# Residual rows loaded behind a one-column memset, and the first product's additions moved into the second product, in a two-layer encoder trunk on one core

## The chip, the core and the metric

The kernel runs on one core of a Trainium2 chip. The core has five engines that run side by side: TensorE (PE in the profile, with PEld for its weight loads), VectorE (DVE), ScalarE (ACT), GpSimd (POOL) and SyncE (SP). SP and POOL issue the transfers here; SP's go through the hardware queue, POOL's through the software queue. The metric is the time of one execution on the device in microseconds: a median of 2541.53 us over three runs (2537.37 to 2542.77).

## The reference

The trunk has two post-norm layers on 1024 positions of width 1024. After each mixer and after each SwiGLU stands a product, a scaled residual and a layer norm; these four places are what the change is about:

```python
    for layer in range(DEPTH):
        if layer % 2 == 0:
            y = even_mixer(x, ...)      # latent attention + Fourier mixing, @ w_out
        else:
            y = odd_mixer(x, ...)       # gMLP spatial gating, @ odd_w_out
        x = layer_norm(DN_ALPHA * x + y, mix_ln_g[layer], mix_ln_b[layer])
        x = layer_norm(DN_ALPHA * x + swiglu(x, ...), ffn_ln_g[layer], ffn_ln_b[layer])
```

`y` is (pages of width 1024) @ (weights): 12 pages of 128 rows for the even mixer, 16 for the odd one, 22 for each SwiGLU. Everything is float32.

## The kernel before

Each of the four products `x = LN(ALPHA * resid + H @ W)` is one call of `reduce` (lines 409 to 594): mix (stage "mix"), ffn0, odd and ffn1, in that order. The product is made from 2x2 blocks with seven half-size products instead of eight, each called a pass p; `source` (line 382) says which sums of pages and of weights a pass multiplies. The page sums SA, SB and weight sums TA, TB are made earlier and kept in device memory (`job`, `direct`, `page_sums`). A float32 matmul is done as three (`mm3`, lines 141 to 143) on operands split into a high part (`xoh`, a cast on ScalarE, line 135) and a low part (`xol`, a subtraction on VectorE, line 136).

Passes run in the order 1, 5, 6, 4, 7, 2, and 3 at the end. A pass has n groups of up to two pages; (p, g) is group g of pass p, and n is 3 in mix, 4 in odd and 6 in ffn0 and ffn1, where the first group has one page. `load(p, g)` brings both sides of a group with SP transfers into six `rx` buffers and splits them into six pairs of cells; then four row blocks s of 128 rows each take 6 matmuls of 512 columns. A group of two pages is 24 matmuls. The first two groups of pass 1 are loaded before the call (`lead`).

The residual rows go into eight tiles `xt[half, s]` of 128x1024 (512 KB each), named x, q, q, y for half 0 and x four times for half 1. Their tags are those of tiles that the stage before has just used: q is TA and TB, x is the last pages and their sums SA and SB. `residual` loads them with POOL transfers; `gained` multiplies them by the last norm's gain and adds its bias (lines 469 and 470, not in mix); `add` adds a product from a PSUM bank (line 457 for the first addition, which scales by ALPHA, line 459 for the others).

The order on each engine is set by a scheduler that takes instructions by priority (in the order of the code) as soon as its own model has them ready; the engine then runs them in that order and waits at the first that is not ready. `behind(mark)` holds an instruction behind a mark in that order; `self.marks[2]` is the VectorE half of the last split of the stream. A transfer issued by POOL whose tile is still being read holds POOL's queue; a VectorE instruction that writes such a tile holds VectorE's.

Of the kernel before, what the change touches and what calls it, by code (L numbers as in the profile page):

```python
# [112 lines left out]
class Trunk:  # L113
# [295 lines left out]
    def reduce(self, st, resid, rgb, ln, keep, pre=None, left=()):  # L409


        nc, a = self.nc, self.a
        lo, hi = self.LO, self.HI
# [3 lines left out]
        n = len(groups)  # L417
# [16 lines left out]
        token = lambda half, s: s // 2 * 4 + half * 2 + s % 2  # L434
        xt = {(1, s): self.m_tile("x") for s in range(4)}
# [4 lines left out]
        def load(p, g):  # L440
            if (p, g) not in ops:
                ops[p, g] = self.stream(st, p, groups[g], raws, pairs)

        def mm(p, g, s):
            if p in (6, 7):
                acc[p, s] = acc[1 if p == 6 else 6, s]
            elif (p, s) not in acc:
                acc[p, s] = self.bank((4 if p in (1, 3) else 0) + s)
            (hh, hl), (uh, ul) = ops[p, g]
            for i, m in enumerate(groups[g]):  # L450
                c, r = slice(i * 512 + s * P, i * 512 + (s + 1) * P), slice(i * 512, (i + 1) * 512)
                self.mm3(acc[p, s], (hh[:, c], hl[:, c]), (uh[:, r], ul[:, r]), m == 0 and p not in (6, 7), m == M - 1, p in (6, 7))

        def add(half, s, c, p, first=False, op=ALU.add):
            x = xt[half, s][:, c]
            if first:
                nc.vector.scalar_tensor_tensor(x, x, ALPHA, acc[p, s], ALU.mult, op)
            else:
                nc.vector.tensor_tensor(x, x, acc[p, s], op=op)

        def residual(half):
            for s in range(4):
                nc.gpsimd.dma_start(xt[half, s], resid[token(half, s)])

        def gained(half, s):
            if rgb is not None:
                x = xt[half, s]
                with self.behind(self.marks[2]):
                    nc.vector.tensor_tensor(x, x, rg, op=ALU.mult)
                    nc.vector.tensor_tensor(x, x, rb, op=ALU.add)  # L470

        def stat(half, s, c):
            if (half, s) not in stats:
                stats[half, s] = self.small.tile([P, 2, 6], F32, tag="st", name=self.name("st"))
            nc.vector.bn_stats(stats[half, s][:, c, :], xt[half, s][:, c * 512:(c + 1) * 512])  # L475
# [43 lines left out]
        def normed1(s):  # L519
            for c in range(2):  # L520
                stat(1, s, c)
            norm(1, s)


        def spread(jobs, k, of):
            i0, i1 = len(jobs) * k // of, len(jobs) * (k + 1) // of
            for j in jobs[i0:i1]:
                j()
        slots = range(4)
        for p in (1, 5, 6, 4, 7, 2):  # L530
            for g in range(n):
                load(p, g)
                if p == 1 and g == 1:
                    load(1, 2)
                    if rgb is not None:
                        rg, rb = (self.bcast(tmp(), a["ln_" + x][rgb[0], rgb[1]]) for x in "gb")
                    residual(0)
                    last = self.job(st, M - 1, True) if st is self.stage["mix"] else None
                if p == 5 and g == 0:
                    residual(1)  # L540
                if p == 6 and g == 0 and keep is None:
                    fg, fb = (self.bcast(self.raw_tile(), a["ln_" + x][ln[0], ln[1]]) for x in "gb")
                if p == 4 and g == 0 and pre is not None:
                    with self.behind(*self.marks):
                        pre()
                if p in (1, 5) and g > 1:
                    spread([lambda s=s: gained(p == 5, s) for s in slots], g - 2, n - 2)
                if p == 2:
                    spread([lambda s=s: normed1(s) for s in slots], g, n)
                for s in slots:  # L550
                    mm(p, g, s)
                    if p == 1 and s % 2 == 1 and left:
                        left.pop(0)()
                    if g == n - 1:
                        if p == 1:
                            add(0, s, lo, p, True)
                        elif p == 5:
                            add(0, s, hi, p, True)
                            add(1, s, hi, p, True)
                        elif p == 6:  # L560
                            add(0, s, hi, p)
                        elif p == 4:
                            add(1, s, lo, p, True, ALU.subtract)
                        elif p == 7:
                            add(1, s, lo, p)
                            add(1, s, hi, p)
                        else:
                            add(0, s, lo, p)
                            stat(0, s, 0)
                if (p, g) == (5, 0) and last is not None:  # L570
                    last(self.marks[2])
# [837 lines left out]
```

## Time and profile before

| | us |
|---|---|
| median of three runs | 2541.53 |
| the profiled execution | 2541.83 |
| its span | 2540.0 |
| PE busy | 2456.4 (97%) |
| DVE busy | 1808.9 (71%) |
| ACT busy | 1111.1 (44%) |
| POOL busy | 318.5 (13%) |

The span is 1.83 us shorter than the execution's own time. Busy PE counts matmuls that overlap in its pipeline, so 97% does not say how often TensorE waits; the chain and the timeline do. The four calls of `reduce` take their first groups near 560 us (mix), 1122 (ffn0), 1690 (odd) and 2304 (ffn1). Times in the rows are microseconds from the start of the span.

### The profile page before, as it was taken

The numbers are of one execution on the slowest core, as the hardware profiler recorded it, in microseconds if no ns is written. First come the engines' busy times: TensorE is split into PE (matmuls) and PEld (weight loads), VectorE is DVE, ScalarE is ACT, GpSimd is POOL, SyncE is SP. The second block draws the span as 40 slices with busy tenths as digits, with TensorE's granted clock in tenths as the row PEclk, the third lists the DMA queues.
The fourth block names the chain that finished last, engine by engine and source line by source line (L and its number), as shares of the span: only waits on it lengthen the run. The fifth ranks groups of instructions, "written<-read, shape, count | busy, mean of one in ns | idle before, by whom it ended". The sixth has DMA issues, their size and how long they took to land.

```text
span 2540.0 us, 33155 instructions
## 1 busy us (share of the span) xinstructions
PE 2456.4 (97%) x12294; PEld 2073.4 (82%) x12294; DVE 1808.9 (71%) x2537; ACT 1111.1 (44%) x1711; POOL 318.5 (13%) x527
## 2 busy tenths in 40 slices
PE   8989999998999999999999999988989999999997
PEld 6778888887878888887889998877878888887885
DVE  4348878767886776768678776768777676677667
ACT  3235555544553333333456446653463333333331
POOL 1000111010111111110002132430011111111001
PEclk9999999998999999999999999999999999999998
DMA  4122333138334444467654554667624444549553
GB/s 175 43 89 71 130 110 125 57 138 282 138 118 174 169 168 162 168 252 251 226 182 172 202 203 137 195 244 276 224 73 163 177 166 155 177 164 329 190 188 140
DMA packets 164329, 431.95 MB, mean 170 GB/s; under 512 B 20136, under 2 KB 26952, under 8 KB 164168
## 3 DMA queue, kind: packets, MB, share of 16 engines
q1 hardware_dynamic: 108216, 232.11, 27.8%
q0 software_dynamic: 55952, 197.73, 20.9%
q8 instruction: 96, 1.57, 0.2%
q14 instruction: 65, 0.53, 0.1%
HBM read 286.64 MB, written 138.41 MB: 167 GB/s over the span
## 4 chain that ended last, share of the span: by engine, by line
PE 81%; DVE 6%; issue 5%; DMA 4%; ACT 2%; POOL 1%; SPq 1%; DVEq 0%; ACTq 0%; POOLq 0%
PE b L142 18%; PE b L141 18%; PE b L143 18%; PE S L1316 6%; PE b L912 5%; PE mm L141 4%; PE mm L142 4%; PE mm L143 4%; PE mm L1335 2%; DVE xol L136 1%; DMA rx<-h 1%; PE b L848 1%; DMA x<-xs 1%; ACT xoh L135 1%; DVE st L475 1%
## 5 line engine op out<-in xcount | busy, mean ns | idle before, releaser
L135 ACT CAST whi<-raw 128x1024 fp32r<-128x1024 f32 (+3 forms) x277 | 261.2, 951 | 383.4 <-PE b L142 240.2
L135 ACT CAST xoh<-rx 128x1024 fp32r<-128x1024 f32 (+1 forms) x252 | 244.5, 1011 | 413.5 <-PE b L142 308.8
L141 PE MATMUL b<-xoh,whi 128*128 128x512 f32 x1040 | 410.7, 396 | 7.9 <-ACT xoh L135 7.9
L136 DVE TENSOR_TENSOR wlo<-raw,whi 128x1024 fp32r<-128x1024 f32 (+3 forms) x277 | 303.4, 1099 | 159.3 <-ACT whi L135 157.1
L142 PE MATMUL b<-xol,whi 128*128 128x512 f32 x1040 | 406.8, 391 | 0.0
L143 PE MATMUL b<-xoh,wlo 128*128 128x512 f32 x1040 | 406.4, 391 | 0.0
L136 DVE TENSOR_TENSOR xol<-rx,xoh 128x1024 fp32r<-128x1024 f32 (+1 forms) x252 | 287.6, 1168 | 166.0 <-ACT xoh L135 160.3
L142 PE MATMUL b<-xol,xoh 128*128 128x512 f32 x960 | 379.4, 395 | 22.3 <-DVE xol L136 22.3
L141 PE MATMUL b<-xoh 128*128 128x512 f32 x960 | 376.1, 394 | 8.5 <-ACT xoh L135 8.5
L143 PE MATMUL b<-xoh,xol 128*128 128x512 f32 x960 | 377.5, 393 | 0.0
L141 PEld LDWEIGHTS b<-xoh,whi 128*128 128x128 f32 x1040 | 196.6, 189 | 50.3 <-ACT xoh L135 8.8
L142 PEld LDWEIGHTS b<-xol,xoh 128*128 128x128 f32 x960 | 183.1, 191 | 63.3 <-DVE xol L136 25.5
L143 PEld LDWEIGHTS b<-xoh,wlo 128*128 128x128 f32 x1040 | 196.3, 189 | 41.3
L142 PEld LDWEIGHTS b<-xol,whi 128*128 128x128 f32 x1040 | 196.5, 189 | 40.4 <-issue 0.5
L141 PEld LDWEIGHTS b<-xoh 128*128 128x128 f32 x960 | 182.9, 190 | 47.6 <-ACT xoh L135 9.3
L143 PEld LDWEIGHTS b<-xoh,xol 128*128 128x128 f32 x960 | 183.1, 191 | 38.2
L663 ACT COPY y<-b 128x512 f32<-128x512 f32 x200 | 116.6, 585 | 192.7 <-PE b L143 186.1
L141 PE MATMUL b<-xah,whi 128*128 128x512 f32 x416 | 162.5, 391 | 1.3 <-ACT xah L135 1.3
L142 PE MATMUL b<-xal,whi 128*128 128x512 f32 x416 | 162.0, 389 | 0.0
L143 PE MATMUL b<-xah,wlo 128*128 128x512 f32 x416 | 161.9, 389 | 0.0
L131 DVE TENSOR_TENSOR raw<-raw,raw 128x512 f32<-128x512 f32 (+1 forms) x174 | 128.5, 739 | 28.2 <-DMA raw<-w_up 24.7
L708 DVE TENSOR_TENSOR y<-b,y 128x512 f32<-128x512 f32 x84 | 58.0, 690 | 82.9 <-PE b L143 82.6
(378 smaller groups left out, 4590.9 us busy)
## 6 DMA issues: line engine op xcount, KB each, us to landing
raw<-w_gate SPq DMA_DIRECT2D x44, 512.0 KB, 3.6
raw<-w_up SPq DMA_DIRECT2D x44, 512.0 KB
q<-w_down POOLq DMA_DIRECT2D x44, 512.0 KB, 5.3
h<-x POOLq DMA_DIRECT2D x44, 512.0 KB, 3.7
rx<-h SPq DMA_DIRECT2D x60, 256.0 KB, 3.0
rx<-w_down SPq DMA_DIRECT2D x60, 256.0 KB, 4.3
raw<-o_v SPq DMA_DIRECT2D x16, 512.0 KB, 6.1
x<-o_out POOLq DMA_DIRECT2D x16, 512.0 KB, 5.7
```

Of the source, the lines that this page charges most:

```text
L131: self.nc.vector.tensor_tensor(out, a, b, op=ALU.subtract)
L135: a = self.nc.scalar.copy(hi, src)
L136: return a.ins, self.nc.vector.tensor_tensor(lo, src, hi.bitcast(F32), op=ALU.subtract).ins
L141: mm(ps, lh, rh, start=start, stop=False, skip_group_check=skip)
L142: mm(ps, lh, rl, start=False, stop=False, skip_group_check=skip)
L143: mm(ps, ll, rh, start=False, stop=stop, skip_group_check=skip)
L475: nc.vector.bn_stats(stats[half, s][:, c, :], xt[half, s][:, c * 512:(c + 1) * 512])
L663: nc.scalar.copy(t, ps)
L708: self.last_v = nc.vector.tensor_tensor(sb, ps, sb, op=op).ins
L912: nc.tensor.matmul(ps[:, i * 256:(i + 1) * 256], l[:, b, k, c], r[:, k, :], start=start and k == 0 and i == 0 and m == 0, stop=k == 3 and ...
L1316: nc.tensor.matmul(sc[:, kb, :], l[:, s], r[:, kb * 512:(kb + 1) * 512], start=i == 0, stop=i == 4)
L1335: nc.tensor.transpose(ps[:, k, :], p[:, kt * P:(kt + 1) * P], self.ident)
```

## The change

```diff
-        def residual(half):
-            for s in range(4):
-                nc.gpsimd.dma_start(xt[half, s], resid[token(half, s)])
+        def residual(half, s):
+
+            with self.behind(self.marks[2]):
+                nc.vector.memset(xt[half, s][:, 0:1], 0.0)
+            nc.gpsimd.dma_start(xt[half, s], resid[token(half, s)])
...
-                    residual(0)
                     last = self.job(st, M - 1, True) if st is self.stage["mix"] else None
-                if p == 5 and g == 0:
-                    residual(1)
+                if p == 1 and 0 < g < 3:
+                    for s in (2 * g - 2, 2 * g - 1):
+                        residual(0, s)
+                if (p == 1 and g == n - 1) or (p == 5 and g == 0):
+                    for s in (0, 1) if p == 1 else (2, 3):
+                        residual(1, s)
...
-                if p in (1, 5) and g > 1:
-                    spread([lambda s=s: gained(p == 5, s) for s in slots], g - 2, n - 2)
+                if p == 1 and g > 1:
+                    spread([lambda s=s: gained(0, s) for s in slots], g - 2, n - 1)
+                if p == 5 and g == 0:
+                    spread([lambda s=s: gained(0, s) for s in slots], n - 2, n - 1)
+                if p == 5 and g > 0:
+                    spread([lambda s=s: gained(1, s) for s in slots], g - 1, n - 1)
+                if (p, g) == (5, 1):
+                    for s in slots:
+                        add(0, s, lo, 1, True)
...
                     if g == n - 1:
-                        if p == 1:
-                            add(0, s, lo, p, True)
-                        elif p == 5:
+                        if p == 5:
                             add(0, s, hi, p, True)
                             add(1, s, hi, p, True)
...
-                        else:
+                        elif p == 2:
                             add(0, s, lo, p)
                             stat(0, s, 0)
```

Each load of a residual row block now follows a memset of its tile's first column on VectorE, which `behind` puts after the splits of the group at hand; the load overwrites the column. There are 32 memsets, eight in a call, on line 464; the loads stand on line 465 and `gained` on 471 and 472 of the changed kernel. The first additions of pass 1 move from the end of pass 1 to the start of group (5, 1).

On VectorE in ffn0, before, from the multiplication of the first row block on (q_9756 and q_9757 are row blocks (0,1) and (0,2), x_9755 is (0,0); the splits of rx_9879 and rx_9884 are those of group (1, 4), the ones of rx_9915 and rx_9920 those of (1, 5)):

```order
L469 TENSOR_TENSOR q_9756<-q_9756,gb_9785 128x1024
L320 TENSOR_TENSOR x_9736<-x_9715,x_9735 128x512
L470 TENSOR_TENSOR q_9756<-q_9756,gb_9787 128x1024
L469 TENSOR_TENSOR x_9755<-x_9755,gb_9785 128x1024
L136 TENSOR_TENSOR xol<-rx_9879,xoh 128x1024
L470 TENSOR_TENSOR x_9755<-x_9755,gb_9787 128x1024
L136 TENSOR_TENSOR xol<-rx_9884,xoh 128x1024
L469 TENSOR_TENSOR q_9757<-q_9757,gb_9785 128x1024
L136 TENSOR_TENSOR xol<-rx_9915,xoh 128x1024
```

The same place in the changed kernel (the row block (0,0) is x_9763, the splits of (1, 4) are those of rx_9889 and rx_9894, of (1, 5) those of rx_9925 and rx_9930):

```order
L464 MEMSET x_9763 128x1
L136 TENSOR_TENSOR xol<-rx_9889,xoh 128x1024
L320 TENSOR_TENSOR x_9744<-x_9723,x_9743 128x512
L136 TENSOR_TENSOR xol<-rx_9894,xoh 128x1024
L471 TENSOR_TENSOR q_9764<-q_9764,gb_9793 128x1024
L472 TENSOR_TENSOR q_9764<-q_9764,gb_9795 128x1024
L136 TENSOR_TENSOR xol<-rx_9925,xoh 128x1024
L471 TENSOR_TENSOR x_9763<-x_9763,gb_9793 128x1024
L136 TENSOR_TENSOR xol<-rx_9930,xoh 128x1024
L472 TENSOR_TENSOR x_9763<-x_9763,gb_9795 128x1024
```

Both splits of (1, 4) now stand ahead of every multiplication, and the one of (0,0) stands between the two splits of (1, 5). On POOL the load of (0,0), which stood ahead of the stores of SA and SB, stands behind both. ffn1 has the same order.

On VectorE in odd, before, from the last page sum on (line 457 is the first addition of pass 1 for the four row blocks; rx_15031 is the second split of group (5, 0), whose first stood fourteen rows earlier, rx_15068 and rx_15073 are (5, 1), rx_15102 is (5, 2)):

```order
L320 TENSOR_TENSOR x_14624<-x_14624,x_14623 128x512
L457 SCALAR_TENSOR_TENSOR x_14828<-x_14828,b_14832 128x512
L457 SCALAR_TENSOR_TENSOR q_14829<-q_14829,b_14839 128x512
L457 SCALAR_TENSOR_TENSOR q_14830<-q_14830,b_14858 128x512
L457 SCALAR_TENSOR_TENSOR y_14831<-y_14831,b_14865 128x512
L136 TENSOR_TENSOR xol<-rx_15031,xoh 128x1024
L136 TENSOR_TENSOR xol<-rx_15068,xoh 128x1024
L136 TENSOR_TENSOR xol<-rx_15073,xoh 128x1024
L136 TENSOR_TENSOR xol<-rx_15102,xoh 128x1024
```

The changed kernel there (rx_15047 is the second split of (5, 0), with the first right ahead of it, rx_15088 the first of (5, 1); x_14842 is row block (1,2), whose tile is read by the store of SA until it has landed):

```order
L136 TENSOR_TENSOR xol<-rx_15047,xoh 128x1024
L317 TENSOR_TENSOR x_14640<-x_14639,x_14640 128x512
L471 TENSOR_TENSOR q_14845<-q_14845,gb_14926 128x1024
L318 TENSOR_TENSOR x_14639<-x_14639 128x512
L472 TENSOR_TENSOR q_14845<-q_14845,gb_14928 128x1024
L319 TENSOR_TENSOR x_14639<-x_14640,x_14639 128x512
L471 TENSOR_TENSOR q_14846<-q_14846,gb_14926 128x1024
L320 TENSOR_TENSOR x_14640<-x_14640,x_14639 128x512
L472 TENSOR_TENSOR q_14846<-q_14846,gb_14928 128x1024
L471 TENSOR_TENSOR y_14847<-y_14847,gb_14926 128x1024
L464 MEMSET x_14842 128x1
L136 TENSOR_TENSOR xol<-rx_15088,xoh 128x1024
```

The splits of (5, 0) now stand ahead of the page sums and of the multiplications, and those of (5, 1) behind them and behind two memsets. Further on, the eight additions of pass 5 stand ahead of both splits of (6, 0), where before one split stood ahead of them and the other after the fourth.

On TensorE in mix, before, at the end of group (5, 1) (b_5738, b_5745, b_5752 and b_5759 are the banks of pass 5 for row blocks 0 to 3, b_5626 is the one of passes 1 and 6 for row block 0):

```order
L143 MATMUL b_5759<-xoh,xol 128x512
L141 MATMUL b_5626<-xoh 128x512
L141 MATMUL b_5738<-xoh 128x512
L142 MATMUL b_5738<-xol,xoh 128x512
L141 MATMUL b_5745<-xoh 128x512
L142 MATMUL b_5745<-xol,xoh 128x512
L141 MATMUL b_5752<-xoh 128x512
```

The changed kernel there (b_5742, b_5749, b_5756 and b_5763 are the banks of pass 5, b_5626, b_5633, b_5640 and b_5647 those of passes 1 and 6):

```order
L143 MATMUL b_5763<-xoh,xol 128x512
L141 MATMUL b_5626<-xoh 128x512
L142 MATMUL b_5626<-xol,xoh 128x512
L143 MATMUL b_5626<-xoh,xol 128x512
...
L141 MATMUL b_5647<-xoh 128x512
L141 MATMUL b_5742<-xoh 128x512
L142 MATMUL b_5742<-xol,xoh 128x512
L141 MATMUL b_5749<-xoh 128x512
```

One matmul of (6, 0) stood ahead of those of (5, 2); now 19 of its 24 do. On VectorE the first additions of pass 1 stand behind the splits of (5, 0) and of (5, 1) there, and all eight memsets behind those of (1, 2).

## Rows read from the trace of the kernel before

**Rows 1.** The page: the chain that ended last, by engine.
```profile
PE 81%; DVE 6%; issue 5%; DMA 4%; ACT 2%; POOL 1%; SPq 1%; DVEq 0%; ACTq 0%; POOLq 0%
```

**Rows 2.** Timeline of PE: start, duration, instruction [idle before it <-what ended it].
```profile
572.08 0.79 PE L141 MATMUL b<-xoh 128*128 128x512 f32 x1 [3.53 <-ACT xoh L135]
...
597.85 0.80 PE L141 MATMUL b<-xoh 128*128 128x512 f32 x1 [4.96 <-ACT xoh L135]
...
1147.44 0.79 PE L142 MATMUL b<-xol,xoh 128*128 128x512 f32 x1 [5.67 <-DVE xol L136]
...
1224.69 0.50 PE L142 MATMUL b<-xol,xoh 128*128 128x512 f32 x1 [0.94 <-DVE xol L136]
...
1701.16 0.79 PE L848 MATMUL b<-q,whi 128*128 128x128 f32 x2 [8.93 <-ACT whi L839]
...
1735.58 0.79 PE L142 MATMUL b<-xol,xoh 128*128 128x512 f32 x1 [6.55 <-DVE xol L136]
...
2328.05 0.79 PE L142 MATMUL b<-xol,xoh 128*128 128x512 f32 x1 [5.18 <-DVE xol L136]
...
2496.12 0.65 PE L142 MATMUL b<-xol,xoh 128*128 128x512 f32 x1 [1.80 <-DVE xol L136]
```

**Rows 3.** Timeline of PE in ffn0, before and after its wait.
```profile
1141.15 0.39 PE L143 MATMUL b<-xoh,xol 128*128 128x512 f32 x1
1141.38 0.39 PE L141 MATMUL b<-xoh 128*128 128x512 f32 x1
...
1149.31 0.63 PE L143 MATMUL b<-xoh,xol 128*128 128x512 f32 x1
1149.74 0.63 PE L141 MATMUL b<-xoh 128*128 128x512 f32 x1
```

**Rows 4.** Timeline of DVE in ffn0.
```profile
1142.76 1.23 DVE L469 TENSOR_TENSOR x<-x,gb 128x1024 f32<-128x1024 f32 x1 [4.64 <-DMA x<-xs]
1143.90 1.22 DVE L136 TENSOR_TENSOR xol<-rx,xoh 128x1024 fp32r<-128x1024 f32 x1
```

**Rows 5.** Timeline of POOL in ffn0.
```profile
1132.68 0.53 POOL L463 DMA_DIRECT2D x<-xs  x1
...
1137.28 0.54 POOL L349 DMA_DIRECT2D ffn0SB<-x  x1 [1.65 <-DVE x L320]
```

**Rows 6.** DMA queues, 1135 to 1139: packets, MB, share of 16 engines.
```profile
q0 software_dynamic: 303, 1.11, 67.9%
q1 hardware_dynamic: 304, 0.56, 36.1%
```

**Rows 7.** Timeline of DVE in ffn1.
```profile
2323.37 1.23 DVE L469 TENSOR_TENSOR x<-x,gb 128x1024 f32<-128x1024 f32 x1 [4.53 <-DMA x<-xs]
```

**Rows 8.** DMA issues, 1137.6 to 1138: KB, us from issue to landing.
```profile
ffn0SB<-x POOLq DMA_DIRECT2D x1, 512.0 KB, 8.6
```

**Rows 9.** Timeline of DVE in odd.
```profile
1726.10 0.69 DVE L317 TENSOR_TENSOR x<-x,x 128x512 f32<-128x512 f32 x1 [1.93 <-DMA tp<-x]
...
1732.51 1.28 DVE L457 SCALAR_TENSOR_TENSOR q<-q,b 128x512 f32<-128x512 f32 x2
1733.70 0.69 DVE L457 SCALAR_TENSOR_TENSOR y<-y,b 128x512 f32<-128x512 f32 x1
```

**Rows 10.** Timeline of ACT in mix.
```profile
570.98 1.04 ACT L135 CAST xoh<-rx 128x1024 fp32r<-128x1024 f32 x1 [2.06 <-DMA rx<-w_out]
...
596.75 2.94 ACT L135 CAST xoh<-rx 128x1024 fp32r<-128x1024 f32 x3 [8.47 <-DMA rx<-mixSB]
```

**Rows 11.** DMA queues, 566 to 572.
```profile
q0 software_dynamic: 402, 1.51, 61.7%
q1 hardware_dynamic: 537, 0.98, 42.4%
```

**Rows 12.** Timeline of POOL in mix.
```profile
587.99 0.54 POOL L341 DMA_DIRECT2D mixSB<-raw  x1 [1.19 <-DVE raw L320]
```

**Rows 13.** Timeline of POOL in odd.
```profile
1732.30 0.54 POOL L862 DMA_DIRECT2D oddSB<-x  x1 [1.20 <-DVE x L320]
...
1735.50 0.53 POOL L463 DMA_DIRECT2D x<-xs  x1 [1.26 <-DMA oddSB<-x]
```

## The prediction, made before the result was known

> **What bounds the kernel now.** First the chain on the page: TensorE carries 81% of it [rows 1], so a time changes only where TensorE waits. Then TensorE's timeline, read for idle time ahead of a matmul. In the four calls of `reduce` (I call them mix, ffn0, odd, ffn1 after their stage) six long waits stand [rows 2]: mix 3.53 and 4.96 us, ffn0 5.67, odd 8.93 and 6.55, ffn1 5.18. After a wait of 1.8 us or more the matmuls come 0.43 us apart instead of 0.23 [rows 3], which is 1.2 GHz instead of 2.4; after one of 0.94 us they do not stay slow [rows 2]. About nine matmuls are slow each time, 9 x 0.2 + 0.2 = 2.0 us. So the six waits cost 34.8 us and 12 us of slow clock with them.
>
> Why they wait, in ffn0: VectorE's `gained` multiply of row block (0,0) stood 4.64 us for its load, and the split that TensorE needed stands right behind it [rows 4]. The load was issued at 1132.68 [rows 5], landed at 1142.7. In that stretch the software queue (POOL's) and the hardware queue (SP's) together fill the 16 engines: shares 67.9% and 36.1% [rows 6]. ffn1 has the same wait, 4.53 us [rows 7].
>
> **ffn0 and ffn1.** The change puts `gained` of (0,0) one group later: behind both splits of group (1,4), as the second order piece shows, so (1,4) runs without a wait. But its load now stands behind the stores SA and SB on POOL, issued with SB at 1137.3 instead of 1132.7 [rows 5]: seventh in the software queue instead of fifth. That queue moves 1.11 MB in 4 us, 278 GB/s, 1.89 us for 524 KB [rows 6]. So it lands at 1142.7 + 2 x 1.89 = 1146.5 (from below: SB, seventh today, landed 8.6 us after its issue, 1145.9 [rows 8]; from above: rival A).
> The second split of (1,5) stands behind that multiply: 1146.5 + 1.14 + 1.23 = 1148.9 (spacing of two such VectorE rows: 1.14 [rows 4]). TensorE wants it after 24 matmuls of (1,4) and one more: 1141.4 + 25 x 0.227 = 1147.05. New wait 1.85 us. Then VectorE has nine instructions of 1024 columns, two of 512 (0.60 each [rows 9]) and four memsets from the landing to the second split of (5,1): 9 x 1.14 + 2 x 0.6 + 4 x 0.1 = 11.9, so 1158.4. No row shows a memset of one column: between 0 and the 0.60 of a 512-wide instruction; I take 0.1, near the low end. Today that point of TensorE comes 60 matmuls after 1147.44: 1147.44 + 60 x 0.227 + 2.0 = 1163.06. Now it comes at 1158.4, or at 1159.1 if the 1.85 us also slow the clock. Gain 4.0 to 4.7, I take 4.4.
> ffn1 by the same steps: landing 2323.3 + 3.8 = 2327.1, split 2329.5, TensorE there at 2328.05 - 5.18 + 24 x 0.227 = 2328.3, wait 1.2 us, no slow clock; VectorE's chain ends at 2339.0, today 2328.05 + 60 x 0.227 + 2.0 = 2343.7. Gain 4.7.
>
> **mix.** Here the splits wait for the stream itself: for the second load of group (1,2), cast at 570.98 [rows 10]. Between 566 and 572 the residual rows on the software queue took 1.51 MB and the stream 0.98 [rows 11]. Seven of the eight row loads now go behind that group's splits. The stream's load has to come 4.8 us earlier to be cast and split (1.05 + 1.24) before TensorE asks at 572.08 - 3.53 = 568.55. With more than half of the traffic ahead of it gone I take that as reached.
> The second wait hangs on the last page's sums: store SB issued at 587.99 [rows 12], the reload cast at 596.75 [rows 10], 8.8 us for a store and a load, 4.4 each. After the change the sums are made earlier (near 577), but the store stands behind eight row loads: issue from 567, first landing near 571, then 524 KB at 1.51 MB per 6 us [rows 11], 2.08 us each, so the eighth at 585.6, SB tenth at 589.8, reload 594.2, TensorE 1.1 later (as 597.85 after 596.75): 595.3. Meanwhile it has (1,2), (5,0), (5,1): 568.55 + 72 x 0.227 = 584.9, and 19 matmuls of (6,0), which the new order puts ahead of (5,2): 589.2. So 6.1 us of wait remain. The end of (5,2) and (6,0): 595.3 + 29 x 0.227 + 2.0 = 603.9, today 597.85 + 47 x 0.227 + 2.0 = 610.5. Gain 6.6. If the software queue had the engines alone (2.49 MB in the 6 us [rows 11], 1.26 us each) SB would be back at 586.7, nothing would wait, end 595.8, gain 14.7. If the first load came no earlier, nothing is gained. I take 8, near the value that rests on today's shares.
>
> **odd.** The 8.93 us wait for ScalarE, which waits for the stream's load; one row load of 512 KB leaves that stretch, 524 KB at 415 GB/s [rows 11] = 1.3 us at most; I take 1. The 6.55 us go: the splits of (5,0) move ahead of the `gained` work (third and fourth order pieces). What is late next: VectorE's work from the page sums on. Its first sum starts at 1726.1, when the store of the page has landed [rows 9]; to the second split of (5,1) there are 4 x 0.6 + 8 x 1.14 + 2 memsets = 11.7, so 1737.8, and TensorE, through (5,0) at 1734.3, waits 3.6. Six more items and four adds bring (5,2) to 1744.7 (wait 1), and the eight adds of pass 5 now stand ahead of both splits of (6,0): 1749.3 + 4 x 1.14 + 8 x 0.6 + 2 x 1.14 = 1761.0, while TensorE arrives at 1755.9: a wait of 5 us and 2 of slow clock, 1763.0. Today the same matmul comes 96 after 1735.58: + 21.8 + 1.6 = 1759.0. So 4 lost, 1 gained: +3. Between -6 (nothing of the chain is late) and +7 (the two new memsets between the sums and the split also wait for stores SA and SB; today such a store took 3.2 us [rows 13], which they just pass).
>
> **The 32 memsets, the doubled adds and the line moves** cost nothing else: the number of `gained` and add instructions is the same; 32 x 0.1 = 3 us on VectorE, which is busy 71%; where they sit in its queue they are priced above.
>
> **Sum.** 8 + 4.4 + 4.7 - 3 = 14.1. The profiled execution took 2541.83, its span 2540.0 and 1.83 around it; the median of the runs is 2541.53, so it needs no correction. 2541.8 - 14.1 = 2527.7, I say 2528.
>
> **Rivals.**
> A. The wait only moves to a later load (no change). The splits of (1,4) are made earlier in ffn0, so their buffers come free and SP refills the hardware queue at once. If the software queue then had half the bytes, 205 GB/s, 2.56 us each: the first of the seven lands at 1142.7 - 4 x 1.89 = 1135.1, the seventh six later at 1150.5, VectorE's chain ends at 1162.4, today 1163.06: 0.6 gained, the same in ffn1. In mix SB would be tenth at 571 + 9 x 2.56 = 594, restart 599.5, gain 2.4. With odd at +3 the time is 2541. Against it: both queues had work in 1135 to 1139, and the software queue still had two thirds of the bytes [rows 6]. The Trainium skill, "DMA: Bandwidth & Descriptors", section "Queues, rings and completion order", says that a DMA engine serves its queues in turn, a whole packet from one before it goes to the next, which speaks for A if packets are alike. In the row the numbers of packets are alike and the packets are not: 303 carried 1.11 MB and 304 carried 0.56 MB [rows 6]. By that rule a busy hardware queue keeps its third and no more, and here the trace agrees.
> B. The order fits better than my chains: odd loses no time at its new places (-8: 6.55 and 1.6 of slow clock), mix comes near its 14.7. Half of that on top of the forecast: (11 + 6.7) / 2 = 9 more, and 2 in the ffns, near 2517. For it: the chains assume that VectorE is never ahead. Against: the eight adds ahead of the splits stand in the order.
> C. Slower. A memset holds VectorE until the earlier reader of its tile is done, and that is a store in three calls (TA and TB, then h, SA, SB; in odd SA and SB). Today POOL stood there, with nothing of the stream behind it. If those stores land as late as SB in ffn0, 8.6 us [rows 8] instead of 3.2 [rows 13], each of the three calls holds VectorE 5 to 7 us more: 3 x 7 = 21, 2549. It is slower once each call is held by more than 5 us. Against it: in the ffns most memsets stand after the landing of those stores.
>
> **Numbers.** Forecast 0.66 (2520 to 2536), A 0.13 (2541), B 0.12 (2517), C 0.09 (2549). What a measurement here can tell from no change is 0.2%, 5.1 us: faster is below 2536.4. Forecast almost whole, B whole and a little of A: 0.79 faster; A's rest and the edge of the forecast: 0.13 same; 0.08 slower. The range 2513 to 2540 leaves out C, half of A and the far end of B.
>
> **What would show it.** In ffn0 and ffn1 no wait at (1,4) and one of 1 to 2 us at (1,5), on a split behind L471; row (0,0) landing 9 us or so after its issue. In mix no wait before group (1,2), matmuls of (6,0) ahead of (5,2), and a wait there below 7 us. In odd the 6.55 us gone, about 3.6 at (5,1) and 5 at (6,0). It is wrong if VectorE's longest idle times end at L464, or if the row loads land later than 1150 in ffn0.

## The result and the profile after

The changed kernel takes 2526.47 us (median of four runs, 2524.29 to 2528.25), the kernel before beside it 2539.69 (2537.37 to 2542.77): 13.2 us less, ratio 0.9947 (95% interval 0.993 to 0.9964). The forecast was 2528. Measured a second time it took 2527.51 (ratio 0.9953, 0.9939 to 0.9967). The profiled execution took 2524.29, its span is 2522.3. Against the 2540.0 of before that is 17.7 less: the profiled execution of before lies 2.1 us above its median here and this one 2.2 below, so sizes of parts are read from the profile with 2 us or so in doubt.

The chain on the page is still TensorE's, as [rows 1]:

```profile
PE 82%; DVE 6%; issue 5%; DMA 4%; ACT 2%; SPq 1%; POOL 0%; DVEq 0%; ACTq 0%; POOLq 0%
```

The waits of TensorE in the same four calls, as [rows 2] has them of before (the matmul's start, its duration, in brackets the idle time ahead of it and what ended it):

```profile
597.11 0.79 PE L141 MATMUL b<-xoh 128*128 128x512 f32 x1 [6.82 <-ACT xoh L135]
...
1143.15 0.50 PE L142 MATMUL b<-xol,xoh 128*128 128x512 f32 x1 [1.10 <-DVE xol L136]
...
1152.47 0.50 PE L142 MATMUL b<-xol,xoh 128*128 128x512 f32 x1 [0.86 <-DVE xol L136]
...
1687.73 0.80 PE L858 MATMUL b<-q,whi 128*128 128x128 f32 x2 [6.73 <-ACT whi L849]
...
1724.23 0.80 PE L142 MATMUL b<-xol,xoh 128*128 128x512 f32 x1 [3.19 <-DVE xol L136]
...
1747.31 0.80 PE L142 MATMUL b<-xol,xoh 128*128 128x512 f32 x1 [3.09 <-DVE xol L136]
...
2318.79 0.50 PE L142 MATMUL b<-xol,xoh 128*128 128x512 f32 x1 [1.62 <-DVE xol L136]
...
2328.10 0.50 PE L142 MATMUL b<-xol,xoh 128*128 128x512 f32 x1 [0.84 <-DVE xol L136]
...
2479.99 0.50 PE L142 MATMUL b<-xol,xoh 128*128 128x512 f32 x1 [1.28 <-DVE xol L136]
```

The 3.53 of mix is gone and the wait behind it has grown from 4.96 to 6.82. The 5.67 and 5.18 of the two ffns at group (1,4) are gone. In their place stand 1.10 and 1.62 at (1,5), and 0.86 and 0.84 at (5,1); the matmuls behind all four come 0.23 us apart, so no slow clock follows them in this profile. Odd has two waits of 3 us in place of the 6.55, each with the slow clock behind it (granted clock 0.50 between 1725 and 1729).

In ffn0, VectorE and POOL at the place of [rows 4] and [rows 5]:

```profile
1134.20 1.22 DVE L136 TENSOR_TENSOR xol<-rx,xoh 128x1024 fp32r<-128x1024 f32 x1
1140.73 1.23 DVE L471 TENSOR_TENSOR x<-x,gb 128x1024 f32<-128x1024 f32 x1 [5.31 <-DMA x<-xs]
1141.87 1.22 DVE L136 TENSOR_TENSOR xol<-rx,xoh 128x1024 fp32r<-128x1024 f32 x1
```
```profile
1131.05 0.54 POOL L349 DMA_DIRECT2D ffn0SB<-x  x1 [1.21 <-DVE x L320]
1131.58 0.53 POOL L465 DMA_DIRECT2D x<-xs  x1
```

Row (0,0) is loaded behind the store SB and lands 9.1 us after its issue; VectorE still stands 5.31 us for it, but now only the second split of (1,5) is behind it, not the splits of (1,4).

The kernels in the table are those of the experiments below. "The tie" is the memset that ties a row's load to the place behind the splits, with the new places of the loads; "additions" stands for the moved first additions and the moved `gained` work. Where the time went, from the timelines of all kernels run here: five TensorE instructions that each kernel has (the last of attention, and one behind each call: at 675.66, 1224.69, 1873.23 and 2496.12 in the kernel before) cut the span into stretches. The numbers are the length of a stretch less that of before, in us; a negative one is a gain.

| kernel | to attention's end | mix | ffn0 | odd | ffn1 | end | median |
|---|---|---|---|---|---|---|---|
| changed | -0.8 | -4.4 | -5.3 | +0.5 | -6.2 | -1.6 | 2526.5 |
| changed, again | -1.5 | -3.5 | -4.8 | +2.8 | -6.0 | -1.6 | 2527.5 |
| tie alone | 0.0 | -4.9 | -6.4 | +0.5 | -6.8 | -1.6 | 2522.7 |
| tie alone, again | -0.2 | -3.5 | -7.2 | +0.1 | -7.9 | -1.6 | 2521.8 |
| additions alone | -0.1 | -2.1 | -3.5 | +1.3 | -5.2 | -1.6 | 2531.4 |
| odd as before | -0.5 | -3.6 | -5.0 | +1.2 | -6.1 | 0.0 | 2526.5 |
| mix rows late | +4.1 | -2.3 | -4.8 | +2.8 | -5.9 | -1.6 | 2529.4 |
| mix rows early | +0.4 | -3.0 | -6.1 | +0.9 | -7.9 | -1.6 | 2524.8 |
| less VectorE in odd | -0.3 | -4.2 | -6.0 | -2.9 | -6.0 | -1.6 | 2518.9 |
| odd late | -1.7 | -4.1 | -6.0 | -3.1 | -7.3 | -1.6 | 2518.8 |
| odd late, (0,0) last | -2.9 | -3.9 | -5.8 | -5.7 | -8.8 | -1.6 | 2516.7 |

The first column is the same code in every kernel, and the spread in it is chance. Two executions of one kernel differ by up to 2.3 us in a stretch (odd of the changed kernel). The stretches are those of the profiled execution, which can lie off the median of its kernel: it was 4.9 us above it for "mix rows late" (2534.28, the longest of its five) and 3.3 below it for "odd late, (0,0) last" (2513.38, the shortest).

### The profile page after: what moved, and what is told of

It is laid out like the page before. It is cut to its first block, busy times and chain, and to the rows that moved or that the text cites. A ratio compares the mean times of both kernels' runs of the same rounds, so it can differ in the third digit from the quotient of the medians.

```text
span 2522.3 us, 33179 instructions
## 1 busy us (share of the span) xinstructions
PE 2451.2 (97%) x12294; PEld 2069.2 (82%) x12294; DVE 1809.0 (72%) x2569; ACT 1111.7 (44%) x1711; POOL 317.7 (13%) x527
## 4 chain that ended last, share of the span: by engine, by line
PE 82%; DVE 6%; issue 5%; DMA 4%; ACT 2%; SPq 1%; POOL 0%; DVEq 0%; ACTq 0%; POOLq 0%
PE b L142 18%; PE b L143 18%; PE b L141 18%; PE S L1326 6%; PE b L922 5%; PE mm L141 4%; PE mm L142 4%; PE mm L143 4%; PE mm L1345 2%; DVE xol L136 2%; PE b L858 1%; SPq L396 1%; DMA rx<-h 0%; DMA rx<-w_down 0%; ACT xoh L135 0%
```

## The experiments

**The tie alone** (from the changed kernel; the code is cut at the dots):

```diff
-                if p == 1 and g > 1:
-                    spread([lambda s=s: gained(0, s) for s in slots], g - 2, n - 1)
...
-                if (p, g) == (5, 1):
-                    for s in slots:
-                        add(0, s, lo, 1, True)
+                if p in (1, 5) and g > 1:
+                    spread([lambda s=s: gained(p == 5, s) for s in slots], g - 2, n - 2)
...
+                        if p == 1:
+                            add(0, s, lo, p, True)
```

> The tie alone: the row loads stand behind a memset behind the splits as in the changed kernel, and gained and the first additions stand where they stood before. My theory: the tie is what moves the waits, since it sets both when the row loads start and what stands ahead of the splits. In ffn0 and ffn1 the multiply of row (0,0) still stands between the two splits of group (1,5), so both calls keep their gain (5.3 and 5.0 us of the 13.2); mix keeps the 3.5 us of its first wait; in odd the four first additions stand again ahead of the second split of (5,0), so its wait of about 6.5 us is back: 2526.5 + 1 to 3 = 2527 to 2530. Rival: the moved additions carry the gain, and the tie only makes loads later: 2537 to 2540, with the waits of 5 us back in ffn0 and ffn1.

Measured: 2522.68 us (0.9938, 0.9926 to 0.9951). My theory held in the ffns and in mix: both calls keep their gain, and the first wait of mix is gone. In odd the wait at the second split of (5,0) is back, with 8.00 us instead of 6.5, and the stretch still takes what it takes in the changed kernel. The whole is faster than I expected, and faster than the changed kernel. So both were measured once more, side by side.

> The changed kernel once more, beside the others of this call, since the tie alone came out at 2522.7 us and the changed kernel at 2526.5 us from another call: 2525 to 2528. If the moved additions cost nothing, it is within 0.1% of the tie alone here; if they cost what the first call shows, it is 3 to 4 us slower.

> The tie alone once more (gained and the first additions where they stood before): 2521 to 2525. Theory that the moved additions are worth nothing on top of the tie: within 0.1% of the changed kernel in this call. Rival that they cost VectorE time ahead of splits: 3 to 4 us faster than it.

Measured: changed 2527.51 (2524.78 to 2529.04), tie alone 2521.76 (2520.20 to 2523.55). The runs do not overlap: the moved `gained` work and additions cost some 5 us on top of the tie. The table shows 1.1 and 2.4 of this in ffn0, 0.6 and 1.9 in ffn1, and 0 and 2.8 in odd. In ffn0, VectorE of the tie alone (second profile):

```profile
1135.31 1.22 DVE L471 TENSOR_TENSOR q<-q,gb 128x1024 f32<-128x1024 f32 x1
1136.56 1.23 DVE L472 TENSOR_TENSOR q<-q,gb 128x1024 f32<-128x1024 f32 x1
...
1141.51 1.23 DVE L471 TENSOR_TENSOR x<-x,gb 128x1024 f32<-128x1024 f32 x1 [2.59 <-DMA x<-xs]
```

The same place of the changed kernel (second profile):

```profile
1140.98 1.23 DVE L471 TENSOR_TENSOR x<-x,gb 128x1024 f32<-128x1024 f32 x1 [6.73 <-DMA x<-xs]
...
1144.41 1.22 DVE L471 TENSOR_TENSOR q<-q,gb 128x1024 f32<-128x1024 f32 x1
...
1146.15 1.22 DVE L472 TENSOR_TENSOR q<-q,gb 128x1024 f32<-128x1024 f32 x1
```

Spread over one group more, the `gained` work of a q row that has landed moves from VectorE's idle time ahead of (0,0) to behind it: VectorE idles 6.73 us (5.31 in the first profile) instead of 2.59, and has two instructions, 2 x 1.14 us, more to do afterwards. The four first additions are through at 1155.1 instead of 1153.2, though the row landed 0.5 us earlier. TensorE pays for this at (5,1): the waits of 0.86 and 0.84 us there in the changed kernel's first profile, and one of 0.86 in ffn1 of its second, do not stand in the tie alone, 1.0 us each. The rest of the 5 us is not that. In ffn0 of the second profiles nearly the whole difference arises at (1,5), where the same multiply and the same split stand in both kernels:

```profile
1143.93 0.50 PE L142 MATMUL b<-xol,xoh 128*128 128x512 f32 x1 [1.36 <-DVE xol L136]
```
```profile
1143.40 0.50 PE L142 MATMUL b<-xol,xoh 128*128 128x512 f32 x1 [2.30 <-DVE xol L136]
```

The first is of the tie alone and has no slow matmul behind it, the second is of the changed kernel and has seven. In the first profiles that wait was the shorter one in the changed kernel (1.10 against 1.52). So about 1 us a call in the ffns is shown to come from the order; why the whole comes to 5 is open.

**The additions alone** (no memsets, the loads at the groups of before):

```diff
-            with self.behind(self.marks[2]):
-                nc.vector.memset(xt[half, s][:, 0:1], 0.0)
...
+                if (p, g) in ((1, 1), (5, 0)):
+                    for s in slots:
+                        residual(p == 5, s)
```

> The moved gained work and additions alone: the row loads stand where they stood before and no memset is there. The order on VectorE already has both splits of (1,4) in ffn0 and ffn1 ahead of the multiply of row (0,0), and its load starts as early as before. If the gain of ffn0 and ffn1 comes from that order, they keep about 5 us each, with a wait of at most 1 to 2 us at (1,5). In mix the row loads go beside the stream again, so the wait of 3.5 us at (1,2) is back and mix is within 2 us of before. Odd as the changed kernel or up to 3 us better, since no memset waits for a store. Sum: 2540 - 10 - 1 + 0 = 2529, 2526 to 2532. Rival (only the tie keeps the loads out of the stream's way, in every call): waits of 4 to 6 us in ffn0 and ffn1 again, 2537 to 2540.

Measured: 2531.37 us (0.9975, 0.9964 to 0.9985), inside my range. Part of ffn0's gain comes without the tie, as the multiply of (0,0) then stands behind the splits of (1,4) too. But all four instructions of (0,0) and of a q row, which waits for nothing, stand ahead of both splits of (1,5):

```profile
1140.51 1.23 DVE L468 TENSOR_TENSOR x<-x,gb 128x1024 f32<-128x1024 f32 x1 [4.96 <-DMA x<-xs]
1141.65 1.22 DVE L468 TENSOR_TENSOR q<-q,gb 128x1024 f32<-128x1024 f32 x1
1142.79 1.22 DVE L469 TENSOR_TENSOR x<-x,gb 128x1024 f32<-128x1024 f32 x1
1143.92 1.22 DVE L469 TENSOR_TENSOR q<-q,gb 128x1024 f32<-128x1024 f32 x1
1145.06 2.35 DVE L136 TENSOR_TENSOR xol<-rx,xoh 128x1024 fp32r<-128x1024 f32 x2
```

TensorE waits 2.70 us there (at 1147.47), and 7 matmuls are slow. The two halves of the change do the same thing in the ffns, and do not add.

In mix my expectation failed: the first wait did not come back, and mix gains 2.1. The loads are not quite where they were. Their line now stands behind the one that loads the last page (`self.job`), and POOL issues the first row at 561.28, behind that page, where the kernel before issued it at 548.81:

```profile
560.75 0.54 POOL L335 DMA_DIRECT2D raw<-mix  x1 [12.00 <-DMA mix<-page]
561.28 0.53 POOL L462 DMA_DIRECT2D x<-x  x1
```

Between 560 and 566 the software queue then moved 0.34 MB and the stream 1.36, where it was 1.37 and 0.85 in the kernel before. So what removes the first wait of mix is that the rows start later, and a move of one line does it without a memset. The wait for the reload of SB is longer than before, 7.75 us at 595.46.

**Odd as before** (memsets, positions and moved additions only where `st is not self.stage["odd"]`):

> The changed kernel with odd alone as before (no memsets, loads, gained and additions in the old places in that call). My theory: the change loses about 1 us in odd (its wait of 6.55 us became two of 3.2 and 3.1, each with slow matmuls behind it): 2525.5, 2523 to 2527, and the 8.9 us wait ahead of odd's first matmuls of spatial work is back to 8.9 from 6.7. Rival: what odd gives is a gain, since the 8.93 us wait shrank by 2.2: then this kernel is slower than the changed one by 2 to 4 us, 2528 to 2531.

Measured: 2526.49 us (0.9948, 0.9936 to 0.9961). The waits of odd are back at 8.11 and 6.67 us, and the kernel takes what the changed one takes. In odd the change is worth less than can be told: even this kernel, with the order of before there, is 1.2 us above the kernel before in that stretch.

**VectorE's load in odd** (the kernel leaves out the gain and bias of half 1 there):

```diff
-            if rgb is not None:
+            if rgb is not None and not (half == 1 and st is self.stage["odd"]):
```

> The changed kernel without the eight gained instructions of half 1 in odd (the gain and bias of that half of the residual are left out of the result). Theory: VectorE has work without a break from the page sums to (6,0), so its work sets odd's later wait: 8 x 1.14 = 9.1 us less of it take away the wait of 3.1 us at (6,0) and the slow clock behind it, the one of 3.2 us at (5,1) stays since it stands behind the page sums: 4 to 5 us faster than the changed kernel, 2521 to 2523. Rival: the stream's transfers or a later wait set odd's end, and nothing is gained: 2525 to 2527.

Measured: 2518.90 us (0.9923, 0.991 to 0.9937), 8.6 less than the changed kernel beside it, more than the 4 to 5 expected. In odd itself the table gives 3.4 to 5.7 us, as the theory has it; the rest lies in stretches whose code is the same. The wait at (6,0) is gone. The one at (5,1) did not stay as it was but is longer, 5.51 us:

```profile
1687.17 0.80 PE L858 MATMUL b<-q,whi 128*128 128x128 f32 x2 [6.17 <-ACT whi L849]
...
1725.44 0.80 PE L142 MATMUL b<-xol,xoh 128*128 128x512 f32 x1 [5.51 <-DVE xol L136]
```

The work on VectorE up to that split is the same in both kernels. It starts with the first page sum, which waits for the transfer of the page; in the changed kernel and in this one:

```profile
1711.76 0.69 DVE L317 TENSOR_TENSOR x<-x,x 128x512 f32<-128x512 f32 x1 [3.27 <-DMA tp<-x]
```
```profile
1712.89 0.69 DVE L317 TENSOR_TENSOR x<-x,x 128x512 f32<-128x512 f32 x1 [4.33 <-DMA tp<-x]
```

Here it started 1.1 us later, and TensorE came 1.1 earlier. So the amount of VectorE's work sets the wait at (6,0), and the wait at (5,1) hangs on a transfer and the work behind it.

**Mix: the rows behind the stores.**

```diff
-                if (p == 1 and g == n - 1) or (p == 5 and g == 0):
-                    for s in (0, 1) if p == 1 else (2, 3):
+                if (p, g) in (((5, 1), (5, 2)) if st is self.stage["mix"] else ((1, n - 1), (5, 0))):
+                    for s in (0, 1) if (p, g) in ((1, n - 1), (5, 1)) else (2, 3):
```

> The changed kernel with the four row loads of half 1 in mix moved behind the stores of the last page's sums (to groups (5,1) and (5,2)); nothing else is changed. My theory: the wait of 6.8 us in mix hangs on the store SB, which stood tenth in the software queue behind eight row loads (14.7 us from issue to the reload); with four row loads fewer ahead of it, at about 1.9 us each, it lands 7 us earlier, the wait falls below 1 us and its slow clock of 1.6 us goes too: 2526.5 - 7 = 2519.5, 2517 to 2522. Rival 1: the store is late because the stream's queue has the engines, not for the row loads ahead of it: landing within 2 us of the changed kernel's, 2525 to 2527. Rival 2: the late rows hold the additions of pass 5 and with them the splits of (6,1): a new wait of 3 to 6 us, 2523 to 2526.

Measured: 2529.43 us (0.9964, 0.995 to 0.9978), slower than both theory and rivals; against the changed kernel the intervals overlap, so it is shown that nothing is gained, not that something is lost. The step that I tested came true and the conclusion did not. POOL and SP in this kernel, where mix starts 4.9 us later than in the changed kernel's profile:

```profile
581.22 0.54 POOL L341 DMA_DIRECT2D mixSB<-raw  x1 [0.19 <-issue]
```
```profile
588.97 0.32 SPq L396 DMA_DIRECT2D rx<-mixSB  x1
```

ScalarE and TensorE behind it:

```profile
597.46 2.94 ACT L135 CAST xoh<-rx 128x1024 fp32r<-128x1024 f32 x3 [8.00 <-DMA rx<-mixSB]
```
```profile
598.55 0.79 PE L141 MATMUL b<-xoh 128*128 128x512 f32 x1 [9.59 <-ACT xoh L135]
```

The store lands 7.7 us after its issue instead of 14.7, as expected. But the reload, with the four row loads and the stream beside it, takes 8.5 us to its cast instead of 4.4. And the scheduler, which orders by its own model, now puts that cast ahead of two others (the row stands for three), and TensorE has 72 matmuls of the product ahead of the wait instead of 91: it runs dry 19 x 0.227 = 4.3 us sooner. Moving the loads moved more than the loads.

**Mix: the rows at the top of the call** (tie alone otherwise, no memsets in mix):

> The tie alone, but in mix the eight row loads stand at the top of the call, ahead of the last page's load on POOL, without memsets. Theory: what is left in mix (waits of about 6 us in all in the run with the tie alone) comes from 4 MB of rows that share the engines with the stream between 566 and 591 (software queue two thirds of the bytes); issued from about 547 on, where the engines are less than 30% busy, they are out of the way: SB's store lands within 4 us and no wait above 1.5 us stays in mix, 4 to 6 us faster than the tie alone: 2517 to 2519. Rival: the tiles are still held by the stage before and the loads hold up POOL's queue, so the last page's sums come later: the waits stay or grow, 2522 to 2528.

Measured: 2524.79 us (0.9943, 0.9931 to 0.9956), the rival. POOL's queue:

```profile
549.25 0.53 POOL L535 DMA_DIRECT2D x<-x  x1
558.25 1.05 POOL L535 DMA_DIRECT2D q<-x  x2 [8.47 <-PE mm L143]
...
563.03 0.53 POOL L335 DMA_DIRECT2D raw<-mix  x1 [1.14 <-DMA mix<-page]
...
589.77 0.54 POOL L341 DMA_DIRECT2D mixSB<-raw  x1 [0.18 <-issue]
```

The second row waits until attention has read the memory that its tile takes over; the seven then share the engines with the stream again (1.67 MB of the software queue between 566 and 572 against 0.83), and the 3.62 us wait ahead of (1,2) is back. The kernel is 3.0 us slower than the tie alone beside it. Whether mix would be free of waits with the rows out of the way is open; no run here got them out of the way.

**A better order in odd** (tie alone, with this in odd only; half 1 is loaded at (5,1) and (5,2); the code is cut to the added lines):

```diff
+                if odd and (p, g) in ((1, 3), (5, 0), (5, 1)):
+                    for s in {(1, 3): (0,), (5, 0): (1,), (5, 1): (2, 3)}[p, g]:
+                        gained(0, s)
+                if odd and (p, g) == (5, 2):
+                    for s in slots:
+                        add(0, s, lo, 1, True)
+                if odd and p == 6:
+                    spread([lambda s=s: gained(1, s) for s in slots], g, n - 1) if g < n - 1 else None
+                if odd and (p, g) == (6, n - 1):
+                    for s in slots:
+                        add(1, s, hi, 5, True)
```

> The tie alone, with another order in odd only: gained of half 0 is spread over (1,3), (5,0) and (5,1), the first additions follow at (5,2), and the loads, gained work and additions of half 1 wait until (5,1), (5,2) and pass 6, so that nothing of half 1 stands ahead of a split of pass 5. Theory: VectorE's work between the last page sums and (6,0) sets odd's waits; 8 gained instructions and 4 additions (8 x 1.14 + 4 x 0.6 = 11.5 us) leave that stretch for pass 6, where VectorE idles about 3 us a group, and the splits of (5,0) and (5,1) stand ahead of the gained work: the wait of 8.0 us of the tie alone falls to 1 to 3 and its slow clock goes: 4 to 7 us faster than the tie alone, 2515 to 2518. Rival: the page sums (they wait for the stores of the page) hold the splits of (5,1) whatever follows, or pass 6 becomes late: 2520 to 2523.

Measured: 2518.81 us (2518.06 to 2520.53; ratio 0.9925, 0.9912 to 0.9937), some 3 to 4 less than the tie alone had taken; odd is 3.1 to 3.5 shorter than in the tie alone, where I had expected 4 to 7. The wait of 8 us at (5,0) in the tie alone is gone. Two short ones stand later, of 0.95 and 2.81 us:

```profile
1732.98 0.50 PE L142 MATMUL b<-xol,xoh 128*128 128x512 f32 x1 [0.95 <-DVE xol L136]
...
1769.41 0.50 PE L142 MATMUL b<-xol,xoh 128*128 128x512 f32 x1 [2.81 <-DVE xol L136]
```

**Row (0,0) last in the ffns**, on top of that (`for s in ((1, 2, 3, 0) if p == 1 else slots)` in the spread of `gained`):

> The kernel of odd_late, with row (0,0) as the last of half 0 that is gained in ffn0 and ffn1 (rows 1, 2, 3, 0). Theory: the 1.1 to 1.5 us wait at (1,5) in both calls is the landing of row (0,0), about 9 us after its issue; with its multiply one group later VectorE has the other rows to do until it lands, both waits go, and VectorE does not idle more than 1 us there: 1 to 3 us faster than odd_late, 2513 to 2517. Rival: the wait is VectorE's amount of work and not the landing: the same time as odd_late within 1 us.

Measured: 2516.66 us (2513.38 to 2518.93; ratio 0.9919, 0.9905 to 0.9932), the fastest here, faster than the kernel before and the changed one. Against odd_late it is 2.2 us by the medians, with runs that overlap, so this last step is not shown in the time. ffn1 has no wait left at (1,5) and gains 1.5 more. In ffn0 the wait has only moved: 1.72 us at (1,4), whose second split now has four of `gained`'s instructions on q rows ahead of it. VectorE no longer waits for (0,0) there (it is multiplied at 1141.14, right behind a split), so the landing was the cause at (1,5). What holds (1,4) now begins with a landing too, VectorE stands 2.27 us for a q row ahead of those four:

```profile
1129.16 1.23 DVE L471 TENSOR_TENSOR q<-q,gb 128x1024 f32<-128x1024 f32 x1 [2.27 <-DMA q<-xs]
```

## Why the prediction was right, and where not

The path was right in the ffns and in mix. That the number came within 1.5 us is in part luck: errors of opposite sign cancelled. Mix was put 3.6 to 4.5 us too high. Against that the two ffns gave 11.4 and 10.7 where 9.1 was forecast, odd cost 0.5 and 2.8 where it was 3, and 1.6 came at the end, where nothing was forecast (the two numbers are the two profiles of the changed kernel). By the medians the gain is 13.2, 14.1 forecast.

**ffn0 and ffn1: right.** No wait at (1,4); row (0,0) landed 9.1 us after its issue, at 1140.73, which is 1145.9 on the clock of before (this profile runs 0.8 + 4.4 us ahead there), 1146.5 predicted. VectorE's work then ends with the second split of (5,1), where TensorE waits again (0.86 us): 1152.47 is 1157.7 on the clock of before, 1158.4 predicted, and in ffn1 2328.10 is 2338.1, 2339.0 predicted. The wait at (1,5) was 1.10 and 1.62, predicted 1.85 and 1.2; in the second profile 2.30 and 1.14, the former with 7 slow matmuls, so that "after a wait of 1.8 us or more" the clock may or may not fall (see the last section). The gain of 5.3 and 6.2 (4.8 and 6.0) against 4.4 and 4.7. Rival A fell in the row that was to decide it: the software queue kept two thirds of the bytes while the hardware queue had work, between 1130 and 1134 as in [rows 6], and up to 1138:

```profile
q0 software_dynamic: 288, 1.07, 65.3%
q1 hardware_dynamic: 328, 0.59, 38.9%
```

**mix: the mechanism right, the size not.** The term was 8 us, measured 4.4 and 3.5. The first wait went as said, and the 6.1 us of wait expected came out as 6.82. The step that failed is the start of the rows: "issue from 567, first landing near 571". On the clock of before, 0.8 us later than this profile's, the issue was at 568.7, and the third row landed at 579.1 where the forecast has 575.2 (in the second profile, 1.5 us ahead, at 578.6); the landings are read from the additions that wait for them, 578.3 and, for the fourth row, 580.3 on the profile's own clock. Two stretches of the queues show why, 566 to 572 as [rows 11] and the next six us:

```profile
q1 hardware_dynamic: 1147, 2.08, 95.6%
q0 software_dynamic: 144, 0.21, 9.8%
```
```profile
q0 software_dynamic: 452, 1.65, 67.8%
q1 hardware_dynamic: 450, 0.82, 35.6%
```

With the rows out of its way the stream took the engines itself, 2.08 MB where it had 0.98 of before, and the rows moved 0.21 MB where the forecast's rate gives 1.0 from 568 on: about 3 us late, an estimate by that rate. From then on they came as reckoned, 1.9 us each. The store SB was issued at 576.9 as predicted and stood behind all eight; its reload was issued at 591.62 and cast 4.4 us later, so TensorE went on at 597.9 on the clock of before instead of 595.3:

```profile
576.88 0.54 POOL L341 DMA_DIRECT2D mixSB<-raw  x1 [0.68 <-DVE raw L320]
```
```profile
591.62 0.32 SPq L396 DMA_DIRECT2D rx<-mixSB  x1
```
```profile
596.01 1.04 ACT L135 CAST xoh<-rx 128x1024 fp32r<-128x1024 f32 x1 [3.85 <-DMA rx<-mixSB]
```

I had then rounded the 6.6 of my chain up to 8, towards a case in which nothing waits; that end had no row behind it. These two, 1.4 and 2.6 us, are about the size of the miss. In the second profile TensorE stood in two places, 1.83 us at 585.21 for a load of the stream and 4.09 at 596.56 for the reload, and went on at the same time, 598.1 on the clock of before. The packets of both queues are alike in number, 450 and 452, and not in bytes. That is what the Trainium skill, "DMA: Bandwidth & Descriptors", section "Queues, rings and completion order", leads to, where an engine takes a whole packet from each queue in turn; the trace agrees.

**odd: the waits right, the size within its doubt.** Predicted 3 lost, measured 0.5 and 2.8, and the kernel with odd as before measured 1.2 there, so that the change loses time in odd is not shown. The waits were 3.19 at (5,1) (3.6 predicted), none at (5,2) (1), 3.09 at (6,0) (5), and the wait of 8.93 shrank by 2.2 instead of 1 (3.68, 3.30 and 1.3 in the second profile). The experiment with less VectorE work supports the working for the wait at (6,0); at (5,1) it shows the transfer of the page as the start of the chain, as the prediction has it.

**The end: not seen.** The 1.80 us wait at 2496.12 [rows 2] is 1.28 and the slow clock behind it is gone, 1.6 us in every changed kernel here but the one with odd as before, where a wait of 1.81 with seven slow matmuls stands there again. Why is open: no edited line acts there.

**The memsets** took 0.06 to 0.07 us each, 0.1 was assumed. The loss of rival C did not come: the longest idle time ahead of one was 1.85 us, in ffn1, with nothing of the stream behind it that was late.

**What the prediction did not ask.** It priced the change as one. It put the place of `gained` one group later down to the change as a whole; the runs show that the tie does it by itself, that the moved work and additions do part of it by themselves, and that together they are 4 to 6 us worse than the tie alone.

## What to carry to other kernels

Where an engine that works in order serves both the stream and late data, put the work on the late data behind the stream's next step in that order (about 5 us a call in the ffns here); then use the idle time ahead of the late data for work whose data is there, instead of pushing that work behind it. When a change has two parts that move the same instruction, price each alone: the second may add only its cost. And in mix the loads that were made to wait let the other queue fill the engines first, so reckon the start of such a load from the end of what the other queue has ready. After moving a load, compare the order of instructions on every engine: the lines moved in two of the experiments changed it on TensorE and on POOL too.

## What the hardware showed that was not expected

The slow clock (0.43 us a matmul instead of 0.23, granted clock 0.50 instead of 1.00, 1.2 GHz instead of 2.4) followed every wait of 3.09 us or more on the stream's splits, and none of 1.05 to 1.72 in ffn0 and ffn1. Between these the length alone does not decide. After 1.80 us eight matmuls were slow in the kernel before and none in the tie alone; after 2.81 us at one place, in two kernels with the same order there, eight and none. Nor does a fast first matmul say that none will be slow: in odd_late the one that ends the wait (0.50 us) and the two behind it are fast. Behind the wait of odd_late, the second of its slow matmuls and the next, 0.43 us apart:

```profile
1770.60 0.63 PE L143 MATMUL b<-xoh,xol 128*128 128x512 f32 x1
1771.03 0.63 PE L142 MATMUL b<-xol,xoh 128*128 128x512 f32 x1
```

and at the same place in the kernel with (0,0) last, 0.23 us apart:

```profile
1767.67 0.50 PE L142 MATMUL b<-xol,xoh 128*128 128x512 f32 x1 [2.81 <-DVE xol L136]
...
1768.71 0.39 PE L143 MATMUL b<-xoh,xol 128*128 128x512 f32 x1
1768.94 0.39 PE L142 MATMUL b<-xol,xoh 128*128 128x512 f32 x1
```

Odd is 2.6 us longer in the first of the two, of which 8 x 0.2 = 1.6 is this.
